# First half of an output projection as seven half-size products, with weight sums added in DRAM

## The chip, the cores and the metric

One core of a Trainium2 chip runs the whole layer. The metric is the device time of one execution in microseconds (us). Names of engines: PE is the matmul engine (PEld its weight load), DVE the vector engine, ACT the scalar engine, POOL and SP the two engines that here mostly issue transfers.

## The reference

One layer of a decoder with three parallel branches (256 positions, width 2048). What matters here is the end: three gated branches are merged, multiplied by a 2048 x 2048 matrix, normalised and added to the input.

```python
def hybrid_layer(x, mem, ...):
    h = rms_norm(x, pre_g)
    proj = h @ w_in
    a_u, a_v, a_g, b_x, b_g, x_q, x_g, gate_logits = jnp.split(proj, splits, axis=-1)
    y_a = spatial_gating(a_u, a_v, ...) * jax.nn.silu(a_g)
    y_b = s5_branch(b_x, ...) * jax.nn.silu(b_g)
    y_x = memory_cross_attention(x_q, rms_norm(mem, mem_g), xa_wk, xa_wv) * jax.nn.silu(x_g)
    ys = jnp.stack([y_a, y_b, y_x], axis=2)
    branch = jnp.einsum('bsnc,ncd->bsnd', ys, w_branch)
    gates = jax.nn.sigmoid(gate_logits.reshape(bsz, seq, N_BRANCH, D_MODEL))
    merged = jnp.sum(gates * branch, axis=2)
    out = merged @ w_out
    return x + rms_norm(out, post_g)
```

`s5_branch` is a state-space layer: a projection of 64 small groups, a scan over the positions, a projection back.

## The kernel before

All matmuls take float32 values split in a high and a low part (type fp32r), and three matmuls (high x high, high x low, low x high) make one product. Activations are split once. Weights stream from DRAM: `load` issues a transfer of 128 x 2048 values (1 MB) on SP's queue into one of three `raw` buffers; `split` makes of each half of it a high part (a cast on ACT, L92) and a low part (a subtraction on DVE, L93), in one of four `hl` buffers; then PE uses them. `tm_quarter` (L215) takes one such 1 MB quarter, 512 rows of a weight by 512 columns, and runs 24 matmuls with 512 columns each: 4 blocks of 128 rows, two halves of the 256 tokens (`tb`), three part products.

PE's instructions stand in the order in which the code is written. On the other engines a scheduler orders the instructions of the whole program by priority and by the time at which its own model sees them ready; each engine then works strictly in that order, and an instruction that waits holds up those behind it.

The layer begins with the state-space input: eight pieces of `start` (x and the first weights) are loaded by SP, then `w_bx`, the query weights `w_xq`, and so on. The state-space work itself (`s5_main`) runs beside the large matmuls: PE's part of it, and the helpers, are issued by `pump` after each block of weights. Its operands come by POOL's queue: `s5_load` loads a block `sb` of 128 KB (L531), `s5_prep` scales it on ACT into `B` (L543), and from the third block on adds its upper half to `B` by an adding transfer (L548):

```python
        a.activation(out=B4, in_=rw, func=AF.Copy, scale=sgn)
        ...
            g.dma_start(out=B4[64:P].bitcast(F32), in_=rw[64:P], accum_op=ALU.add)
```

At the end, the last branch is merged over four column blocks c (`w_br`, 2 quarters each), and `merge_t(c)` transposes the merged rows (`mt`) and splits them into `mm`, 16 blocks of 128 rows by 256 tokens. Then the output projection: three column blocks of 512 (4 quarters each, into one `acc` tile for both token halves), 256 columns from `w_out3[0]` (the 96 narrow matmuls of L1041), and the last 256 columns, whose four half buffers are split while the narrow matmuls run (`wks`; its first quarter in two pairs `wh`, `wl` of 512 columns); they are used by 48 matmuls for token half 0, then 48 for token half 1. `evac_out` squares each result on ACT, for the norm (L1003), and multiplies it by `gpost` on DVE (L1006). After the last square sum, `finish` scales, adds x and sends.

Of the kernel before, what the change touches and what calls it, by code (L numbers as in the profile page):

```python
# [9 lines left out]
F32 = mybir.dt.float32  # L10
# [8 lines left out]
P = 128  # L19
# [24 lines left out]
def trunk(ctx: ExitStack, tc: tile.TileContext, I, out):  # L44
# [109 lines left out]
    class Plain:  # L154
# [5 lines left out]
        def stationary(self, h, tb):  # L160
            return self.t[:, h, tb::2] if self.turn else self.t[:, h, tb * P:(tb + 1) * P]

    def norm_split(src, gv, dst, k0):
        for k in range(len(dst)):
            kk = k0 + k
            r = src[:, k * T:(k + 1) * T].rearrange("p (c b) -> p c b", c=2)
            hi, lo = dst[k].half(0), dst[k].half(1)
            a.activation(out=hi, in_=r, func=AF.Copy, scale=gv[:, kk:kk + 1])
            v.scalar_tensor_tensor(out=lo, in0=r, scalar=gv[:, kk:kk + 1],  # L169
                                   in1=hi.bitcast(F32), op0=ALU.mult, op1=ALU.subtract)  # L170
# [20 lines left out]
        pe.matmul(ps, lhsT=hl.stationary(0, tb), rhs=two(wl), start=False, stop=False)  # L191
        pe.matmul(ps, lhsT=hl.stationary(1, tb), rhs=two(wh), start=False, stop=last)  # L192

    bg = [iter(()), 0.0, []]

    def pump(credit):
        with tc.high_priority(offset=-BEHIND):
# [1 line left out]

    def pump_(credit):  # L200
        bg[1] += credit
        for gen in list(bg[2]):
            while True:
                c = next(gen, "end")
                if c == "end":
                    bg[2].remove(gen)
# [45 lines left out]
    for _ in range(NWARM):  # L252
        pe.matmul(wps, lhsT=wz[:, 0:P], rhs=wz, start=True, stop=True)

    xhl = [Pairs(xp.tile([P, 2, 2, P], F32R, name=f"x{k}")) for k in range(16)]
    u = slot("U", [P, 8, T])
    acc0 = [acc_tile(), acc_tile()]
    for pc in range(8):
# [551 lines left out]
    def merge(n, yhl, sink):  # L810
        for c in range(4):
            rate["tm"] = RT[6] + (0.33, 0.13, 0.0, 0.0)[c] * (n == 2)
            G = acc_tile()
            for kq in range(4):
                tm_quarter([G[:, 0], G[:, 1]], load(I["w_gate"][n, c, kq]), xhl, kq, 16)
            assert not bg[2] or n == 2 and c == 0
            Bp = acc_tile()
            sg = wk.tile([P, 2, 512], F32, tag="w0", name=nm("g"))
            for tb in range(2):
                a.activation(out=sg[:, tb], in_=G[:, tb], func=AF.Sigmoid, scale=rstd_x[:, tb:tb + 1])  # L820
            for kq in range(2):
                tm_quarter([Bp[:, 0], Bp[:, 1]], load(I["w_br"][n, c, kq]), Lane(yhl), kq, 8)
            sink(c, sg, Bp)
# [138 lines left out]
    def mm_tile(i):  # L962
        if i not in mm:
            mm[i] = slot(("H0", "H3", "U", "X0")[i], [P, 4, 2, T], F32R)
        return mm[i]

    def merge_t(c):
        yield None
        yield None
        for hf in range(2):  # L970
            tp = miscp.tile([P, 2, T], F32, tag="misc", name=nm("mt"))
# [6 lines left out]
            split_to(d[:, :, 0], d[:, :, 1], tp)  # L978
            if hf == 0:
                yield None  # L980

    for c in range(4):
        Bp = acc_tile()
        for kq in range(2):
            tm_quarter([Bp[:, 0], Bp[:, 1]], load(I["w_br"][1, c, kq]), yBs, kq, 8)
        for tb in range(2):
            d = sgB[tb][:, csl(c)]
            v.tensor_tensor(out=d, in0=Bp[:, tb], in1=d, op=ALU.mult)
            v.tensor_tensor(out=mg[tb][:, csl(c)], in0=mg[tb][:, csl(c)], in1=d, op=ALU.add)
# [11 lines left out]
    def sq_out(tb, ps, n, cs):  # L1001
        t = wk.tile([P, cs.stop - cs.start], F32, tag="w1", name=nm("sq"), padded_shape=[P, 512])
        a.activation(out=t, in_=ps, func=AF.Square, scale=D ** -0.5, accum_out=ssq[:, tb, n:n + 1])  # L1003

    def gated(dst, ps, lo_, hi_):
        v.tensor_tensor(out=dst, in0=ps, in1=gpost[:, 0, lo_:hi_], op=ALU.mult)  # L1006

    def evac_out(tb, ps, n, cs):
        sq_out(tb, ps, n, cs)
        if tb == 0 or n == 0:  # L1010
            gated(og[tb][:, cs], ps, cs.start, cs.stop)
        elif n == 1:
            gated(held[0], ps, 512, 1024)
        else:
            gated(ps, ps, cs.start, cs.stop)
            held.append(ps)

    held = [yp.tile([P, 512], F32, tag="y", name="held")]
    for n in range(3):
        acc = acc_tile()  # L1020
        for kq in range(4):
            tm_quarter([acc[:, 0], acc[:, 1]], load(I["w_out"][n, kq]), mhl2, kq, 16)
            if (n * 4 + kq) in (1, 4, 7):
                dst, src = late.pop(0)
                nc.sync.dma_start(out=dst, in_=src)
        for tb in range(2):
            evac_out(tb, acc[:, tb], n, csl(n))

    def tm_k(ps, wh, wl, k, tb):
        tm_mm(ps, wh, wl, mhl2[k], tb, k == 0, k == 15)  # L1030

    acc = acc_tile()
    for kh in range(2):
        raw = load(I["w_out3"][0, kh])
        for hf in range(2):
            wh, wl = split(raw[:, hf * 1024:(hf + 1) * 1024])
            for k in range(4):
                kk, ks = kh * 8 + hf * 4 + k, slice(k * T, (k + 1) * T)
                for i, (h, w) in enumerate(((0, wh), (0, wl), (1, wh))):
                    for tb in range(2):  # L1040
                        pe.matmul(acc[:, tb, 0:T], lhsT=mhl2[kk].stationary(h, tb), rhs=two(w[:, ks]),  # L1041
                                  start=kk == 0 and i == 0, stop=kk == 15 and i == 2)
    for tb in range(2):
        evac_out(tb, acc[:, tb, 0:T], 3, slice(1536, 1792))
    v.tensor_reduce(out=ss, in_=ssq[:, :, 0:4], axis=AX.X, op=ALU.add)
    v.tensor_scalar(out=ss, in0=ss, scalar1=EPS, scalar2=None, op0=ALU.add)
    a.activation(out=warm, in_=ss[:, 0:1], func=AF.Sqrt)
# [4 lines left out]
    for kh in range(2):  # L1052
        raw = load(I["w_out3"][1, kh])
        for hf in range(2):
# [147 lines left out]
```

## Time and profile before

| | |
|---|---|
| median of 3 runs | 907.83 us (907.59 to 908.53) |
| profiled execution | 908.71 us, its span 907.0 us |
| mean granted PE clock | 0.997 |
| PE busy | 896.6 us, 4896 matmuls |
| DVE, ACT busy | 760.7 us, 573.0 us |
| loaded and stored | 195.30 MB, mean 215 GB/s |

The span is from the first to the last instruction of the profiled execution. A busy share is an average over stages with different limits. In rows of the trace the first column is the start (or the stretch) in us from the start of the span, then comes the duration, the engine and line, the operation, and what it writes and reads; in brackets is how long the engine was idle before it and whose end it waited for. Rows of PE overlap, since matmuls are pipelined: their pitch is the distance of their starts.

### The profile page before, as it was taken

What the parts mean: (1) busy time and instruction counts of PE and PEld (TensorE: products, weight loads), DVE (VectorE), ACT (ScalarE), POOL (GpSimd) and SP (SyncE); (2) the same over time, 40 slices, a digit from 0 to 9 for tenths busy, and PEclk for the clock granted to TensorE, in tenths of its full rate; (3) what the DMA queues carried; (4) which work ended last, traced back from release to release, by engine and by line L of the source; (5) the groups of instructions that cost most, each with busy time, mean ns of one, the idle gap of its engine ahead of it and who ended that gap; (6) DMA issues with size and microseconds to landing.
All of it is one profiled execution on the core that took longest, in us unless ns stands there. A gap on an engine that the chain in (4) does not pass through costs nothing.

```text
span 907.0 us, 13070 instructions
## 1 busy us (share of the span) xinstructions
PE 896.6 (99%) x4896; PEld 797.2 (88%) x4896; DVE 760.7 (84%) x1188; ACT 573.0 (63%) x980; POOL 50.8 (6%) x80
## 2 busy tenths in 40 slices
PE   8999999999999999999999999999999999999996
PEld 7999898899888888889999888888988889998896
DVE  6899877977887999999797799999997967875554
ACT  7586655876667677685545667777666556544452
POOL 1000000100000111110000001110000000000000
PEclk9999999999999999999999999999999999999998
DMA  9877665653565666765655565566566566557542
GB/s 340 327 280 277 257 240 195 203 185 141 186 201 196 204 225 228 287 203 195 223 195 186 195 203 203 197 205 245 195 216 213 189 236 213 201 186 279 197 175 93
DMA packets 32864, 195.30 MB, mean 215 GB/s; under 512 B 4257, under 2 KB 6817, under 8 KB 11041
## 3 DMA queue, kind: packets, MB, share of 16 engines
q1 hardware_dynamic: 28000, 185.81, 57.4%
q0 software_dynamic: 3936, 6.16, 3.2%
q10 hardware_dynamic: 864, 2.49, 0.7%
q8 instruction: 38, 0.62, 0.3%
q14 instruction: 26, 0.21, 0.1%
HBM read 190.39 MB, written 2.10 MB: 212 GB/s over the span
## 4 chain that ended last, share of the span: by engine, by line
PE 89%; DVE 6%; DMA 2%; issue 1%; ACT 1%; SPq 0%; DVEq 0%; ACTq 0%
PE acc L190 19%; PE acc L192 19%; PE acc L191 19%; PE acc L174 17%; PE acc L179 9%; DVE hl L93 2%; DMA M<-mem 2%; PE acc L1041 1%; PE y L639 1%; PE bu L577 1%; DMA st<-start 1%; DVE H L169 1%; ACT hl L92 1%; PE po L758 1%; PE sc L724 1%
## 5 line engine op out<-in xcount | busy, mean ns | idle before, releaser
L93 DVE TENSOR_TENSOR hl<-raw,hl 128x1024 fp32r<-128x1024 f32 x319 | 388.1, 1220 | 108.7 <-ACT hl L92 107.0
L92 ACT CAST hl<-raw 128x1024 fp32r<-128x1024 f32 x319 | 331.4, 1045 | 210.8 <-PE acc L192 131.0
L174 PE MATMUL acc<-x,hl 128*128 128x512 f32 x736 | 218.7, 383 | 1.0 <-DVE x L169 1.0
L190 PE MATMUL acc<-hl,x 128*128 128x512 f32 x448 | 170.7, 381 | 0.0
L191 PE MATMUL acc<-hl,x 128*128 128x512 f32 x448 | 169.8, 379 | 0.0
L192 PE MATMUL acc<-hl,x 128*128 128x512 f32 x448 | 169.8, 379 | 0.0
L179 PEld LDWEIGHTS acc<-x,hl 128*128 128x128 f32 x736 | 137.0, 190 | 18.9
L179 PE MATMUL acc<-x,hl 128*128 128x256 f32 x736 | 139.0, 274 | 0.0
L174 PEld LDWEIGHTS acc<-x,hl 128*128 128x128 f32 x736 | 113.5, 193 | 2.9 <-ACT hl L92 1.8
L190 PEld LDWEIGHTS acc<-hl,x 128*128 128x128 f32 x448 | 84.7, 189 | 13.6 <-issue 2.5
L192 PEld LDWEIGHTS acc<-hl,x 128*128 128x128 f32 x448 | 84.7, 189 | 12.0
L191 PEld LDWEIGHTS acc<-hl,x 128*128 128x128 f32 x448 | 84.8, 189 | 11.2
L190 PE MATMUL acc<-hl,H 128*128 128x512 f32 (+1 forms) x180 | 68.2, 379 | 0.0
L191 PE MATMUL acc<-hl,H 128*128 128x512 f32 (+1 forms) x180 | 67.8, 377 | 0.0
L192 PE MATMUL acc<-hl,H 128*128 128x512 f32 (+1 forms) x180 | 67.8, 377 | 0.0
L174 PE MATMUL acc<-H,hl 128*128 128x512 f32 x192 | 57.4, 381 | 0.0
L548 POOL DMA_DIRECT2D B<-sb x30 | 25.4, 847 | 452.0 <-ACT B L543 410.8
L383 DVE TENSOR_TENSOR p<-bu,E 128x512 f32<-128x512 f32 x64 | 41.8, 684 | 1.3 <-PE bu L577 1.0
L615 DVE TENSOR_TENSOR_SCAN p<-s5r,p 128x256 f32<-128x256 f32 x64 | 41.3, 681 | 0.6
L179 PEld LDWEIGHTS acc<-H,hl 128*128 128x128 f32 x192 | 36.1, 189 | 5.7 <-DVE hl L93 0.8
L190 PEld LDWEIGHTS acc<-hl,H 128*128 128x128 f32 x180 | 34.0, 189 | 4.9 <-issue 0.4
L192 PEld LDWEIGHTS acc<-hl,H 128*128 128x128 f32 x180 | 34.0, 189 | 4.7
(276 smaller groups left out, 1244.3 us busy)
## 6 DMA issues: line engine op xcount, KB each, us to landing
raw<-w_gate SPq DMA_DIRECT2D x48, 1024.0 KB, 4.8
raw<-w_br SPq DMA_DIRECT2D x24, 1024.0 KB, 4.8
raw<-w_out SPq DMA_DIRECT2D x16, 1024.0 KB, 4.8
raw<-w_xq SPq DMA_DIRECT2D x8, 1024.0 KB, 4.8
raw<-wk SPq DMA_DIRECT2D x8, 1024.0 KB, 4.8
raw<-wv SPq DMA_DIRECT2D x8, 1024.0 KB, 4.8
raw<-w_xg SPq DMA_DIRECT2D x8, 1024.0 KB, 4.9
raw<-w_av SPq DMA_DIRECT2D x8, 1024.0 KB, 5.3
```

What stands on the lines that cost most here:

```text
L92: a.copy(out=hi, in_=src)
L93: v.tensor_tensor(out=lo, in0=src, in1=hi.bitcast(F32), op=ALU.subtract)
L169: v.scalar_tensor_tensor(out=lo, in0=r, scalar=gv[:, kk:kk + 1], in1=hi.bitcast(F32), op0=ALU.mult, op1=ALU.subtract)
L174: pe.matmul(ps, lhsT=wh, rhs=hl.moving_both(), start=k == 0, stop=False)
L179: pe.matmul(h, lhsT=wl, rhs=hl.moving(0), start=False, stop=k == nk - 1)
L190: pe.matmul(ps, lhsT=hl.stationary(0, tb), rhs=two(wh), start=first, stop=False)
L191: pe.matmul(ps, lhsT=hl.stationary(0, tb), rhs=two(wl), start=False, stop=False)
L192: pe.matmul(ps, lhsT=hl.stationary(1, tb), rhs=two(wh), start=False, stop=last)
L383: v.tensor_tensor(out=o, in0=i0, in1=i1, op=op)
L548: g.dma_start(out=B4[64:P].bitcast(F32), in_=rw[64:P], accum_op=ALU.add)
L577: pe.matmul(bu[:, ri, :], lhsT=B4[:, ri, :], rhs=two(U4), start=True, stop=True)
L615: v.tensor_tensor_scan(out=p2[:, ri], data0=rb, data1=p1[:, ri], initial=0.0, op0=ALU.mult, op1=ALU.add)
```

## The change

The first 1024 of the 2048 output columns are computed in another way. Let A be the merged activations (256 tokens by 2048), cut into token halves and row halves of the weight, and B the weight's first 1024 columns, cut into four quarters of 1024 rows by 512 columns. Instead of eight products of quarters there are seven (Strassen's method), each with 128 tokens, 1024 rows and 512 columns: 24 matmuls of 512 columns (`product`). Four of the seven take sums of weight quarters (`wsum`), and four take sums of activation quarters (S1 to S4). The results are put together by additions.

The sums of weights are formed in DRAM by transfers that POOL issues: for each `wsum`, 2 MB, two copies of 1 MB and four adding transfers of 0.5 MB. In the code their generator `weight_sums` is stepped by `pump` from the first `merge` on, with six steps between two transfers. The other 512-column block (`normal`) and the narrow columns (`narrow`) stand between the products. Two products take weight quarters that are loaded early into tiles `xr`, which take the place of the activation tiles `x`; so do `gpost` and x.

```diff
+    dram = ctx.enter_context(tc.tile_pool(name="dram", bufs=1, space=bass.MemoryType.DRAM))
+    wsum = [[dram.tile([P, 2048], F32, name=f"wsum{i}{k}") for k in range(2)] for i in range(4)]
+
+    def weight_sums():
+        w = I["w_out"]
+        for i, (base_, add) in ((0, (w[0, 0:2], w[1, 0:2])), (2, (w[1, 0:2], w[1, 2:4])),
+                                (1, (wsum[2], w[0, 0:2])), (3, (wsum[1], w[0, 2:4]))):
+            for k in range(2):
+                yield from steps(6)
+                g.dma_start(out=wsum[i][k], in_=base_[k])
+            for k in range(2):
+                for c in range(2):
+                    yield from steps(6)
+                    sl = slice(c * 1024, (c + 1) * 1024)
+                    g.dma_start(out=wsum[i][k][:, sl], in_=add[k][:, sl], accum_op=ALU.add)
+
+    bg[3].append(weight_sums())
     merge(2, yX, sink_first)
...
 def merge_t(c):
...
             split_to(d[:, :, 0], d[:, :, 1], tp)
+            lo_, up = tp[:, :, 0:P], tp[:, :, P:T]
+            if c < 2:
+                a.copy(out=r21[:, k], in_=up)
+                v.tensor_tensor(out=r3[:, k], in0=lo_, in1=r21[:, k], op=ALU.subtract)
+                split_to(S3[:, k, 0], S3[:, k, 1], r3[:, k])
+            else:
...
+                tt(t[:, 0], r21[:, k], up, ALU.subtract)
+                stt(t[:, 1], r3[:, k], -1.0, up, ALU.mult, ALU.subtract)
+                tt(t[:, 2], lo_, t[:, 1], ALU.add)
+                split_to(S1[0][:, k, 0], S1[0][:, k, 1], t[:, 0])
...
+    def early(src, i0):
+        ts = [xp.tile([P, 512], F32, tag=f"x{i0 + k}", name=nm("xr")) for k in range(4)]
+        for k in range(4):
+            nc.sync.dma_start(out=ts[k], in_=src[:, k * 512:(k + 1) * 512])
+        return ts
...
     for c in range(4):
         Bp = acc_tile()
         for kq in range(2):
             tm_quarter([Bp[:, 0], Bp[:, 1]], load(I["w_br"][1, c, kq]), yBs, kq, 8)
+        first_raws.append(early(I["w_out"][0, c], 4 * c))
...
-    for n in range(3):
-        acc = acc_tile()
-        for kq in range(4):
-            tm_quarter([acc[:, 0], acc[:, 1]], load(I["w_out"][n, kq]), mhl2, kq, 16)
...
+    def product(ps, form, raws_):
+        for kq in range(2):
...
+                for k in range(2):
+                    kk, sl = kq * 4 + hf * 2 + k, slice(k * 512, (k + 1) * 512)
+                    f = form[kk]
+                    pe.matmul(ps, lhsT=f(0), rhs=two(wh[:, sl]), start=kk == 0, stop=False)
+                    pe.matmul(ps, lhsT=f(0), rhs=two(wl[:, sl]), start=False, stop=False)
+                    pe.matmul(ps, lhsT=f(1), rhs=two(wh[:, sl]), start=False, stop=kk == 7)
+            pump(0.0)
...
+    normal(0)
+    product(X, a11, first_raws[0:2])
+    normal(1)
+    spread("g", I["g_post"][0].broadcast_to([P, D]), 0)
+    normal(2)
...
+    product(Y, a12, first_raws[2:4])
...
+    normal(3)
...
+    product(X, forms(S2[0][:, k] for k in range(8)), wsum[1])
...
+    narrow(0)
...
+    product(Z, forms(S1[0][:, k] for k in range(8)), wsum[0])
...
+    narrow(1)
...
+    product(Y, forms(S3[:, k] for k in range(8)), wsum[2])
...
+    tt(s3, Y, s2, ALU.add)
+    tt(c22, s5, s3, ALU.subtract)
+    sq_out(1, c22, 1, csl(1))
+    gated(held[0], c22, 512, 1024)
+    product(Z, forms(S4[k // 2][:, k % 2] for k in range(8)), w_o[1, 2:4])
+    tt(s5, Z, s5, ALU.add)
+    tt(s5, s5, s2, ALU.subtract)
...
+    product(X, a22, wsum[3])
+    tt(s3, X, s3, ALU.add)
+    sq_out(1, s3, 0, csl(0))
+    gated(og[1][:, csl(0)], s3, 0, 512)
```

Where the scheduler puts these instructions is seen in each engine's order. On POOL, near the start of the program, the rows of before are these (`ones` is a small constant, `sb` the first blocks of the state-space layer, whose first COPY waits for a cast on ACT):

```order
L311 MEMSET ones_1104 128x128
L530 COPY sb_1575<-H_21_363 128x1
L530 COPY sb_1604<-H_21_363 128x1
L531 DMA sb_1575<-s5b 128x256
L531 DMA sb_1604<-s5b 128x256
L531 DMA sb_1648<-s5b 128x256
```

In the change the same MEMSET is followed at once by the transfers of `weight_sums`; 16x16384 is a copy of 1 MB, 128x1024 an adding transfer of 0.5 MB:

```order
L318 MEMSET ones_1104 128x128
L858 DMA wsum_2405<-w_out 16x16384
L858 DMA wsum_2406<-w_out 16x16384
L863 DMA wsum_2405<-w_out 128x1024 x2
L863 DMA wsum_2406<-w_out 128x1024 x2
L858 DMA wsum_2409<-w_out 16x16384
L858 DMA wsum_2410<-w_out 16x16384
```

Then come four more adds, and after them, still on POOL:

```order
L858 DMA wsum_2407<-wsum_2409 16x16384
L858 DMA wsum_2408<-wsum_2410 16x16384
L863 DMA wsum_2407<-w_out 128x1024 x2
L863 DMA wsum_2408<-w_out 128x1024
L537 COPY sb_1575<-H_21_363 128x1
L537 COPY sb_1604<-H_21_363 128x1
L863 DMA wsum_2408<-w_out 128x1024
L538 DMA sb_1575<-s5b 128x256
L538 DMA sb_1604<-s5b 128x256
```

So all 24 transfers moved to the program's start, and `sb` from behind the MEMSET to behind 18 of them. An add waits for the copy into its tile, the copy of a `wsum` tile for the adds to it, and the first two copies wait for nothing. The orders of PE, DVE, ACT and SP are the same as before up to the last stages.

At the end of the program DVE's order before has the splits of the last 256 columns (`wl` twice, then `hl_8306`, `hl_8311` and `hl_8314`) among those of the narrow columns (`hl_8231` and `hl_8258`):

```order
L93 TENSOR_TENSOR hl_8202<-raw_8173,hl_8202 128x1024
L93 TENSOR_TENSOR wl_8299<-raw_8296,wh_8298 128x512
L93 TENSOR_TENSOR wl_8303<-raw_8296,wh_8302 128x512
L93 TENSOR_TENSOR hl_8231<-raw_8229,hl_8231 128x1024
L93 TENSOR_TENSOR hl_8258<-raw_8229,hl_8258 128x1024
L1006 TENSOR_TENSOR M_1023_7738<-acc_8037,gpost 128x512
L93 TENSOR_TENSOR hl_8306<-raw_8296,hl_8306 128x1024
L1006 TENSOR_TENSOR acc_8037<-acc_8037,gpost 128x512
L93 TENSOR_TENSOR hl_8311<-raw_8309,hl_8311 128x1024
L93 TENSOR_TENSOR hl_8314<-raw_8309,hl_8314 128x1024
```

In the change most of them stand behind the addition that reads the last product (`sn_8389<-acc_7821`), and the second `wl` behind the sum of the squares (TENSOR_REDUCE):

```order
L93 TENSOR_TENSOR hl_8471<-raw_8460,hl_8471 128x1024
L390 TENSOR_TENSOR sn_8176<-sn_8176 128x512
L93 TENSOR_TENSOR hl_8499<-raw_8489,hl_8499 128x1024
L1062 TENSOR_TENSOR M_1037_7817<-sn_8176,xr_8001 128x512
L390 TENSOR_TENSOR sn_8389<-acc_7821,sn_8389 128x512
L93 TENSOR_TENSOR wl_8492<-raw_8489,wh_8491 128x512
L93 TENSOR_TENSOR hl_8504<-raw_8502,hl_8504 128x1024
L93 TENSOR_TENSOR hl_8507<-raw_8502,hl_8507 128x1024
L1062 TENSOR_TENSOR M_1038_7818<-sn_8389,xr_8000 128x512
L1171 TENSOR_REDUCE sm_7820<-sm_7819 128x2
L93 TENSOR_TENSOR wl_8496<-raw_8489,wh_8495 128x512
```

The first `wl` has moved behind the last product, the second one to the end of the list; PE needs the second after the first.

More of the change, by code (lines that the diff above doesn't have):

```diff
@@ L192, in tm_mm, with steps @@
         pe.matmul(ps, lhsT=hl.stationary(1, tb), rhs=two(wh), start=False, stop=last)
-    bg = [iter(()), 0.0, []]
+    bg = [iter(()), 0.0, [], []]
+    def steps(n):
+        for _ in range(n):
+            yield None
     def pump(credit):
@@ L201, in pump_ @@
         bg[1] += credit
-        for gen in list(bg[2]):
+        for gens, gen in [(z, gen) for z in bg[2:] for gen in z]:
             while True:
@@ L253, in trunk @@
         pe.matmul(wps, lhsT=wz[:, 0:P], rhs=wz, start=True, stop=True)
-    xhl = [Pairs(xp.tile([P, 2, 2, P], F32R, name=f"x{k}")) for k in range(16)]
+    xhl = [Pairs(xp.tile([P, 2, 2, P], F32R, tag=f"x{k}", name=f"x{k}")) for k in range(16)]
     u = slot("U", [P, 8, T])
@@ L1032, in trunk, with spread, part @@
-    acc = acc_tile()
-    for kh in range(2):
+    post = {}
+    def spread(key, src, i0):
+        post[key] = early(src, i0)
+    def part(key, lo_, hi_):
+        return post[key][lo_ // 512][:, lo_ % 512:(hi_ - 1) % 512 + 1]
+    def gated(dst, ps, lo_, hi_):
+        v.tensor_tensor(out=dst, in0=ps, in1=part("g", lo_, hi_), op=ALU.mult)
+    XY = acc_tile()
+    X, Y = XY[:, 0], XY[:, 1]
+    N = acc_tile()
+    a11 = [mhl2[k].half2(0) for k in range(8)]
+    a12 = [mhl2[k + 8].half2(0) for k in range(8)]
@@ L1034, in trunk, with forms, normal, narrow @@
+    def forms(tiles):
+        return [(lambda h, t=t: t[:, h]) for t in tiles]
+    def normal(kq):
+        tm_quarter([N[:, 0], N[:, 1]], load(I["w_out"][2, kq]), mhl2, kq, 16)
+    c3 = []
+    def narrow(kh):
+        if not c3:
+            c3.extend(bup.tile([P, 512], F32, tag="bu", name=nm("oacc")) for _ in range(2))
         raw = load(I["w_out3"][0, kh])
@@ L1040, in trunk, with snap_tile @@
                     for tb in range(2):
-                        pe.matmul(acc[:, tb, 0:T], lhsT=mhl2[kk].stationary(h, tb), rhs=two(w[:, ks]),
+                        pe.matmul(c3[tb][:, 0:T], lhsT=mhl2[kk].stationary(h, tb), rhs=two(w[:, ks]),
                                   start=kk == 0 and i == 0, stop=kk == 15 and i == 2)
-    for tb in range(2):
-        evac_out(tb, acc[:, tb, 0:T], 3, slice(1536, 1792))
+            pump(0.0)
+    def snap_tile():
+        return wk.tile([P, 2, 512], F32, tag="w0", name=nm("sn"))
@@ new lines, in trunk @@
+    w_o = I["w_out"]
+    normal(0)
[3 more added lines that the diff above has]
+    normal(2)
+    sn = snap_tile()
+    s1, c11 = sn[:, 0], sn[:, 1]
+    a.copy(out=s1, in_=X)
+    product(Y, a12, first_raws[2:4])
+    tt(c11, s1, Y, ALU.add)
+    sq_out(0, c11, 0, csl(0))
+    gated(og[0][:, csl(0)], c11, 0, 512)
+    normal(3)
+    spread(0, I["x"][0], 4)
+    sq_out(0, N[:, 0], 2, csl(2))
+    sq_out(1, N[:, 1], 2, csl(2))
+    gated(og[0][:, csl(2)], N[:, 0], 1024, 1536)
@@ L1064, in trunk @@
                 wks += [(wh[:, k * T:(k + 1) * T], wl[:, k * T:(k + 1) * T]) for k in range(4)]
-    at = [bup.tile([P, 512], F32, tag="bu", name=nm("oacc"))[:, 0:T], acc[:, 1, T:2 * T]]
+    at = [c3[tb][:, T:2 * T] for tb in range(2)]
     ro = small([P, 2])
@@ L1098, in trunk @@
             for hf in halves_:
-                g.tensor_tensor(out=og[1][:, hf], in0=og[1][:, hf], in1=xo[1][:, hf], op=ALU.add)
+                g.tensor_tensor(out=og[1][:, hf], in0=og[1][:, hf], in1=part(1, hf.start, hf.stop), op=ALU.add)
             for hf in halves_:
```

83 lines of the change are left out of this document (52 added, 31 removed).

## The prediction

> **What bounds the kernel now.** I read the page first: the span, who is busy, and by what the chain that ended last is made up.
>
> ```profile
> span 907.0 us, 13070 instructions
> PE 896.6 (99%) x4896; PEld 797.2 (88%) x4896; DVE 760.7 (84%) x1188; ACT 573.0 (63%) x980; POOL 50.8 (6%) x80
> PEclk9999999999999999999999999999999999999998
> PE 89%; DVE 6%; DMA 2%; issue 1%; ACT 1%; SPq 0%; DVEq 0%; ACTq 0%
> ```
>
> TensorE works from end to end at full clock, and the chain is 89% PE. So a matmul taken away is worth its whole pitch, and a pause of PE costs its whole length. The next view, stretches of 10 us, says where there is room for more transfers.
>
> ```profile
> core 0: us, PE busy (x) PEld busy (x) DVE busy (x) ACT busy (x) POOL busy (x), PEclk, DMA share, GB/s
> 0.00:10.00 10.00, 7.58 (x25) 4.63 (x26) 3.18 (x9) 5.17 (x13) 3.29 (x12) 1.00 0.78 246
> 10.00:20.00 10.00, 10.00 (x61) 9.14 (x61) 9.33 (x19) 9.00 (x20) 0.00 (x0) 1.00 1.03 411
> 20.00:30.00 10.00, 10.00 (x64) 9.20 (x63) 7.75 (x13) 7.04 (x12) 0.00 (x0) 1.00 0.99 392
> 30.00:40.00 10.00, 10.00 (x63) 9.21 (x62) 9.52 (x32) 5.58 (x8) 0.00 (x0) 1.00 0.75 273
> 40.00:50.00 10.00, 10.00 (x63) 9.21 (x62) 10.00 (x57) 6.36 (x11) 1.60 (x4) 1.00 0.77 274
> ```
>
> The columns before the last name the share of the 16 DMA engines. From 10 to 30 us they are full, 392 to 411 GB/s; until 50 us they moved 2.46 + 4.11 + 3.92 + 2.73 + 2.74 = 16 MB. This is the stretch into which the change puts its transfers, as the order of POOL shows: all 24 of them stand right behind the MEMSET of `ones`, the first two with nothing to wait for. POOL's rows and ACT's, in order of time:
>
> ```profile
> 3.83 0.21 POOL L311 MEMSET ones<- 128x128 f32 x1
> 45.66 0.30 POOL L530 COPY sb<-H 128x1 f32<-128x1 f32 x2 [41.62 <-ACT H L168]
> 46.16 1.30 POOL L531 DMA_DIRECT2D sb<-s5b  x2 [0.20 <-POOL sb L530]
> 151.91 0.88 POOL L548 DMA_DIRECT2D B<-sb  x1 [49.45 <-ACT B L543]
> ...
> 8.63 0.51 ACT L168 ACTIVATE x<-st,xv 128x256 fp32r<-128x256 f32 x1 [1.44 <-DMA st<-start]
> 13.47 0.51 ACT L168 ACTIVATE x<-H,xv 128x256 fp32r<-128x256 f32 x1 [0.95 <-DMA H<-start]
> 51.61 0.90 ACT L543 ACTIVATE B<-sb,sm 128x256 fp32r<-128x256 f32 x2
> 52.42 1.05 ACT L92 CAST hl<-raw 128x1024 fp32r<-128x1024 f32 x1
> 54.62 1.05 ACT L92 CAST hl<-raw 128x1024 fp32r<-128x1024 f32 x1 [1.15 <-PE acc L179]
> ```
>
> Two things are to be seen. At 8.63 and 13.47 us ACT waits for the start loads, so they have no lead. And at 51.61 us ACT needs `sb`, loaded by POOL at 46.16; behind it on ACT stand the casts without which PE has no weights. In the change ACT's order is the same up to the last stages, but POOL issues `sb` only behind 6 of the 8 copies and all 12 of the adds that belong to them.
>
> **The change part by part.** *Matmuls.* 8 quarters of 24 matmuls become 7 products of 24: 24 fewer. The pitch is that of rows 26 matmuls apart; the last pass has its own:
>
> ```profile
> 782.76 0.38 PE L190 MATMUL acc<-hl,yB 128*128 128x512 f32 x1
> 788.37 0.38 PE L192 MATMUL acc<-hl,yB 128*128 128x512 f32 x1
> ...
> 893.68 0.28 PE L190 MATMUL acc<-wh,H 128*128 128x256 f32 x1
> 898.92 0.28 PE L192 MATMUL acc<-hl,X 128*128 128x256 f32 x1
> ```
>
> (788.37 - 782.76) / 26 = 0.216 us; 24 of them are **-5.2 us**, all on the path. The last pass has 47 steps in 5.24 us, 0.11 each.
>
> *The tail on DVE.* The splits of the last 256 columns stood under the narrow matmuls; now they stand behind the last product. These are the durations:
>
> ```profile
> 782.22 1.22 DVE L93 TENSOR_TENSOR hl<-raw,hl 128x1024 fp32r<-128x1024 f32 x1
> 783.35 1.29 DVE L989 TENSOR_TENSOR M<-M,H 128x512 f32<-128x512 f32 x2
> 875.18 1.29 DVE L93 TENSOR_TENSOR wl<-raw,wh 128x512 fp32r<-128x512 f32 x2 [0.26 <-ACT wh L92]
> 890.39 0.15 DVE L1045 TENSOR_REDUCE sm<-sm 128x2 f32<-128x8 f32 x1
> ```
>
> A 1024 split blocks DVE 1.13 us (783.35 - 782.22), a 512 operation about 0.6. In the new order DVE waits at `sn<-acc` for the last product, then does that (0.6), the first `wl` (0.6), two `hl` (2.3), the gating (0.6), the reduce (0.15) and only then the second `wl` (0.65): 4.9 us. The pass of token half 0 needs the second `wl` after its first 6 matmuls, at about 1.3 + 0.7 = 2.0 us; it then waits to 4.9, and its other 42 matmuls end at 4.9 + 4.7 = 9.6 instead of 5.3. **+4.3 us**; the bounds are 0 (if the scheduled order hardly bites) and 6 (if the last `raw` is late too).
>
> *More splits and sums.* 7 products take 28 splits of 1024 where 16 stood: 12 × 1.13 = 13.6 us of DVE and 12 casts of about 1 us on ACT, and DVE gets some 35 operations of 256 and 512 elements for the factors and sums, about 15 us. In the last stage DVE had this room:
>
> ```profile
> 820.00:840.00 20.00, 20.00 (x98) 17.54 (x97) 10.38 (x10) 9.88 (x13) 0.00 (x0) 1.00 0.76 286
> 840.00:860.00 20.00, 20.00 (x94) 17.50 (x94) 11.00 (x10) 8.83 (x12) 0.00 (x0) 1.00 0.55 207
> 860.00:880.00 20.00, 20.00 (x105) 17.80 (x104) 11.61 (x11) 10.27 (x14) 0.00 (x0) 1.00 0.60 211
> ```
>
> It was busy 33 of 60 us, so 27 were free there, and a little more in the columns of `w_br` before. 29 us just go in; following the order row by row I find PE fed, since four `hl` buffers lie ahead: 0, bounds 0 and 4. If that cover goes, a product takes 4 × 1.13 + 3 × 0.6 = 6.3 us instead of 24 × 0.216 = 5.2.
>
> *Loads at the end.* First products take early tiles, loaded under `glu` and `w_br` by SP: 4 MB more over some 25 us. SP waits there for x tiles that the last gate has read; PE is past them by then. Cost 0, bounds 0 and 2. The later products need 1 MB per 2.6 us, and one such load lands in 4.8:
>
> ```profile
> raw<-w_out SPq DMA_DIRECT2D x16, 1024.0 KB, 4.8
> ```
>
> With three buffers that just holds; 0, bounds 0 and 3.
>
> *The sums in DRAM.* Nothing in before adds in DRAM. The nearest rows are POOL's own transfers, in two short windows (151.9 to 154.8, and 262 to 268 us): packets, MB, share of the 16 engines, then the landing times.
>
> ```profile
> q0 software_dynamic: 80, 0.07, 24.8%
> B<-sb POOLq DMA_DIRECT2D x1, 64.0 KB, 2.6
> ...
> q0 software_dynamic: 48, 0.13, 5.5%
> sb<-s5b POOLq DMA_DIRECT2D x1, 128.0 KB, 3.1
> ```
>
> A plain load of 128 KB occupies the engines 0.055 × 6 = 0.33 us, which is 2.6 us per MB. The adding transfer of 64 KB occupies them 0.248 × 2.9 = 0.72 us: 4 rows of 1 KB on each engine, 0.18 us a row, more than four times the 0.041 of a plain row. A new add has 8 rows of 4 KB per engine. Its lower end is a fixed price per row, 8 × 0.18 = 1.4 us; its upper end a price per byte, 8 × 0.72 = 5.8. I take half of each, 3.6 us, since nothing here separates them. Latency outside the transfer is about 2.6 - 0.7 = 1.9 us.
>
> Until `sb` lands: POOL free at 4.0; five latencies on the chain copy, add, copy, add, load (9.5) and some four issues (0.85 each, 3.4); 6 copies of 1 MB (15.7); 12 adds (43). That is 76 us with the engines to itself. SP's 16 MB take 41 us of the same engines; the chain's own pauses give room for some 17, so 24 more would make 100. Not all of that is needed before ACT's place, and an add that waits on memory may leave the engine to others, so I take **90**. ACT stands at 51.6 then, and PE has a lead: the cast at 54.62 waited for PE to free a buffer of four, so two more halves of 12 × 0.216 = 2.6 us lay between that moment and the use of what was cast at 52.42: it was needed at 59.8, took 2.2 for cast and split, and had 5.2 us to spare. The pause of PE is 90 - 51.6 - 5.2 = **+33 us**. Bounds: with adds at 1.4 us the chain ends between 50 and 74, and at 5.8 between 102 and 126: 0 to 17, and 45 to 69. The two copies and four adds left behind `sb` meet full `raw` buffers: **+2**, bounds 0 and 6.
>
> The Trainium skill, "DMA: Bandwidth & Descriptors", section "Anatomy of one DMA — SWDGE (gpsimd) path", fits such a transfer by 2.0 us plus its bytes at 436 GB/s, with no surcharge for adding. By it an add of 512 KB would be 3.2 us with its latency, and `sb` would land at an estimated 43 us, so ACT would not wait at all. This case's 64 KB add, 0.72 us on the engines where that rate gives 0.15, speaks against it.
>
> Sum against the profiled execution, 908.71 us (0.9 above the median of 907.83): 908.7 - 5.2 + 4.3 + 33 + 2 = 943, about **942** for a median.
>
> **The rivals.** *Starved start.* Adds are cheap (1.4 to 2.4 us) and `sb` lands at 60 to 75, but the start loads, without lead at 8 to 14 us, share full engines with the copies. 4 to 5 MB of POOL's transfers before 30 us, at 2.6 us each, delay PE by 10 to 13 us, and the `sb` wait adds little: 908.7 - 0.9 + 12 to 20, 920 to 928. For it: DMA share 1.03; against it: the dear row of 0.18 us.
>
> *Adds priced per byte.* `sb` lands at 110 to 126, PE pauses 53 to 69: 960 to 980. For it: the 1 KB row ran at only 91 GB/s over 16 engines; against it: part of that must be fixed.
>
> *Not slower.* The added rows run like plain rows and fit between SP's packets: chain 17 + 15.7 + 15.7 = 48 us, `sb` in time. It decides from landing below 57 us (51.6 + 5.2). Then the end stage alone counts: 908.7 - 0.9 = 907.8, or 903.5 if DVE's late `wl` costs nothing. Against it: 12 MB more beside 16 MB at 2.45 us per MB is 70 us by bytes alone.
>
> **How the numbers follow.** The main case (PE waits for ACT's `sb`, adds of 2.4 to 4.8 us, 928 to 960) has 0.50, around 942. The starved start has 0.22, the price per byte 0.23, and not slower 0.05, of which 0.03 faster. The range leaves out the fringe on both sides: 917 to 972. A difference under 0.2% (1.8 us) is about what these runs can't tell from none.
>
> **What would show it.** Right: POOL's adds fill 4 us to beyond 80; ACT waits tens of us on `sb` at its first `B`, with PE idle behind it and DMA share near 1 until then; PE idle about 3 us just after the last pass began; 24 fewer matmuls of 512. Wrong: `sb` lands before 57 us; or PE idle already at 8 to 35 us on `start` and little at `B`; or idle between products, where I put 0.

## The result and the profile after

The changed kernel takes 965.6 us (median of 4 runs, 963.9 to 967.2), beside 908.2 for the kernel before on the same chip (4 runs): a ratio of 1.063, 95% interval 1.061 to 1.066. It is slower, and by 23.6 us more than the 942 predicted. The profiled execution took 967.2 us. First the page's lines that answer to those of before: the span, the engines' busy time, the granted clock and the DMA share in 40 slices, POOL's DMA queue, and what the chain of waits is made of.

```profile
span 965.5 us, 13226 instructions
PE 913.4 (95%) x4872; PEld 806.3 (84%) x4872; DVE 789.5 (82%) x1248; ACT 591.9 (61%) x1022; POOL 68.0 (7%) x104
PEclk9799889999999999999999999999999999999997
DMA  9999986665544656585665565657566588556672
q0 software_dynamic: 6496, 22.94, 9.7%
PE 83%; DMA 11%; DVE 4%; issue 1%; ACT 1%; SPq 0%; POOL 0%; DVEq 0%; ACTq 0%
```

PE has 24 matmuls fewer and is yet busy 16.8 us longer; its granted clock is below 0.9 in slices 2, 5 and 6. DMA is now 11% of the chain, and the DMA row is full for five slices, to about 120 us. The stretches of 10 us from the start say the same in numbers:

```profile
0.00:10.00 10.00, 7.58 (x29) 4.70 (x30) 4.13 (x11) 5.72 (x13) 4.46 (x14) 1.00 0.92 321
10.00:20.00 10.00, 5.65 (x26) 4.91 (x25) 4.16 (x9) 3.87 (x8) 4.41 (x6) 0.83 0.91 302
20.00:30.00 10.00, 5.99 (x30) 5.24 (x29) 2.69 (x5) 1.93 (x4) 0.00 (x0) 0.80 1.03 238
30.00:40.00 10.00, 5.49 (x25) 4.43 (x23) 2.17 (x4) 1.94 (x4) 1.71 (x2) 0.84 1.02 361
40.00:50.00 10.00, 7.25 (x32) 6.34 (x32) 4.34 (x8) 3.87 (x8) 1.65 (x2) 0.67 1.03 284
```

PE was full from 10 us on in before; here it issues 25 to 32 matmuls in 10 us instead of 61 to 64, long before the first `sb` is wanted. Who keeps it waiting is seen in ACT's rows (start, duration, what it waited for), and what POOL does meanwhile in POOL's. A third fence has `memT`'s row in the kernel before, and the time from issue to landing of `w_bx`, before and after:

```profile
15.07 0.51 ACT L171 ACTIVATE x<-st,xv 128x256 fp32r<-128x256 f32 x1 [5.49 <-DMA st<-start]
...
26.00 0.51 ACT L171 ACTIVATE x<-H,xv 128x256 fp32r<-128x256 f32 x1 [6.28 <-DMA H<-start]
...
41.58 0.51 ACT L171 ACTIVATE x<-H,xv 128x256 fp32r<-128x256 f32 x1 [6.95 <-DMA H<-start]
...
72.06 1.99 ACT L92 CAST hl<-raw 128x1024 fp32r<-128x1024 f32 x2 [8.30 <-DMA raw<-w_bx]
...
88.57 0.91 ACT L171 ACTIVATE H<-M,xv 128x256 fp32r<-128x256 f32 x2 [7.09 <-DMA M<-memT]
...
100.11 0.51 ACT L550 ACTIVATE B<-sb,sm 128x256 fp32r<-128x256 f32 x1 [5.88 <-DMA sb<-s5b]
```

```profile
3.97 1.24 POOL L858 DMA_DIRECT2D wsum<-w_out  x2
...
89.14 0.51 POOL L537 COPY sb<-H 128x1 f32<-128x1 f32 x2 [17.28 <-ACT H L171]
...
90.11 1.45 POOL L538 DMA_DIRECT2D sb<-s5b  x2
```

```profile
45.09 0.90 ACT L168 ACTIVATE H<-M,xv 128x256 fp32r<-128x256 f32 x2
...
raw<-w_bx SPq DMA_DIRECT2D x4, 1024.0 KB, 14.5
...
raw<-w_bx SPq DMA_DIRECT2D x4, 1024.0 KB, 40.0
```

ACT waits for `start`, `w_bx` and `memT`, piece after piece, and only at the end 5.9 us for `sb`. The loads' queue tells how late they are: `raw<-w_bx` lands 40.0 us after its issue instead of 14.5, the four `H<-start` 24.0 instead of 10.9 (medians). POOL itself stands 17.3 us at the COPY ahead of `sb`, because ACT's `H` is late. So the wait for `sb` is the last link of a start that was late already.

One place serves as a ruler: POOL's second `ones`, which waits for a matmul (L321 before, L328 after), at 102.25 us before and 156.78 after. The two stretches up to it, of before and of after, hold the same 590 matmuls:

```profile
0.00:102.25 102.25, 99.83 (x590) 89.42 (x591) 90.61 (x265) 68.61 (x117) 5.96 (x18) 1.00 0.82 307
```

```profile
0.00:156.78 156.78, 117.96 (x590) 99.78 (x591) 93.73 (x271) 68.54 (x119) 23.72 (x42) 0.88 0.96 309
```

54.5 us are lost here. PE is idle 38.8 us instead of 2.4 (+36.4), and its busy time for the same work is 18.1 us longer. The granted clock was 0.50 in seven stretches, 37.55 us in all, in which PE was busy 29.41 us: half of that, 14.7 us, is an estimate of what the slow clock cost. What makes up the other 3.4 us of busy time isn't shown. POOL's queue took these shares of the 16 DMA engines in the two stretches:

```profile
q0 software_dynamic: 192, 0.52, 1.6%
```

```profile
q0 software_dynamic: 2752, 17.30, 42.8%
```

The balance of the engines closes: 0.428 x 156.78 = 67.1 us for POOL's queue, 65.5 more than before (0.016 x 102.25 = 1.6); their free time fell from 0.18 x 102.25 = 18.4 to 0.04 x 156.78 = 6.3 us, so 12.1 of it were used; 65.5 - 12.1 = 53.4 us, of 54.5. This is bookkeeping: it says that the other traffic cost nearly what it did before, and not yet why PE is late. The experiments below test that. Nor does a packet's time tell whether the engine itself or the memory behind it was slow.

After that the two programs run in step, 54 us apart, until the last branch; the end adds 4.0 (of 967.2 - 908.7 = 58.5, less 54.5).

The end, in PE's rows around the start of the last pass:

```profile
939.12 0.27 PE L193 MATMUL oacc<-wh,H 128*128 128x256 f32 x1
941.31 0.38 PE L194 MATMUL oacc<-wl,H 128*128 128x256 f32 x1 [1.92 <-DVE wl L93]
...
942.44 0.38 PE L193 MATMUL oacc<-wh,H 128*128 128x256 f32 x1 [0.30 <-ACT wh L92]
944.86 0.58 PE L194 MATMUL oacc<-wl,H 128*128 128x256 f32 x1 [2.04 <-DVE wl L93]
...
945.45 0.42 PE L193 MATMUL oacc<-wh,H 128*128 128x256 f32 x1
...
950.99 0.30 PE L195 MATMUL oacc<-hl,U 128*128 128x256 f32 x1
...
951.47 0.28 PE L193 MATMUL oacc<-hl,X 128*128 128x256 f32 x1
...
951.91 0.28 PE L194 MATMUL oacc<-hl,X 128*128 128x256 f32 x1
```

PE waits 1.92 + 0.30 + 2.04 = 4.3 us, just what was predicted. But from 945.45 to 950.99 the pitch is 0.213 (26 steps in 5.54) instead of the 0.11 of the last four (951.47 to 951.91): from 944.86 on 28 steps took 6.13 us where 3.1 would do, 3.0 us more.

### The profile page after: what moved, and what is told of

Same layout as the page of the kernel before. It is cut to its first block, busy times and chain, and to the rows that moved or that the text cites. A ratio compares the mean times of both kernels' runs of the same rounds, so it can differ in the third digit from the quotient of the medians.

```text
span 965.5 us, 13226 instructions
## 1 busy us (share of the span) xinstructions
PE 913.4 (95%) x4872; PEld 806.3 (84%) x4872; DVE 789.5 (82%) x1248; ACT 591.9 (61%) x1022; POOL 68.0 (7%) x104
## 4 chain that ended last, share of the span: by engine, by line
PE 83%; DMA 11%; DVE 4%; issue 1%; ACT 1%; SPq 0%; POOL 0%; DVEq 0%; ACTq 0%
PE acc L177 17%; PE acc L193 17%; PE acc L194 16%; PE acc L195 16%; PE acc L182 9%; DMA sp<-s5p 4%; DVE hl L93 2%; DMA M<-memT 2%; DMA M<-x 2%; DMA H<-start 1%; PE oacc L1110 1%; DMA sb<-s5b 1%; PE y L646 1%; PE bu L584 1%; PE po L761 1%
## 5 line engine op out<-in xcount | busy, mean ns | idle before, releaser
L177 PE MATMUL acc<-x,hl 128*128 128x512 f32 x736 | 228.2, 397 | 31.4 <-ACT hl L92 15.8
L182 PEld LDWEIGHTS acc<-x,hl 128*128 128x128 f32 x736 | 140.9, 196 | 26.5 <-DVE hl L93 6.6
L177 PEld LDWEIGHTS acc<-x,hl 128*128 128x128 f32 x736 | 118.8, 200 | 35.6 <-ACT hl L92 33.9
L182 PE MATMUL acc<-x,hl 128*128 128x256 f32 x736 | 144.1, 282 | 3.1 <-DVE hl L93 3.1
L177 PE MATMUL acc<-H,hl 128*128 128x512 f32 x192 | 57.4, 381 | 0.0
L193 PE MATMUL acc<-hl,H 128*128 128x512 f32 x144 | 54.9, 382 | 0.0
L194 PE MATMUL acc<-hl,H 128*128 128x512 f32 x144 | 54.6, 379 | 0.0
L195 PE MATMUL acc<-hl,H 128*128 128x512 f32 x144 | 54.6, 379 | 0.0
L182 PE MATMUL acc<-H,hl 128*128 128x256 f32 x192 | 36.9, 274 | 0.0
L193 PEld LDWEIGHTS acc<-hl,H 128*128 128x128 f32 x144 | 27.2, 189 | 4.0 <-issue 0.4
```

Source lines behind the costliest of these rows:

```text
L177: pe.matmul(ps, lhsT=wh, rhs=hl.moving_both(), start=k == 0, stop=False)
L182: pe.matmul(h, lhsT=wl, rhs=hl.moving(0), start=False, stop=k == nk - 1)
L193: pe.matmul(ps, lhsT=hl.stationary(0, tb), rhs=two(wh), start=first, stop=False)
```

## The experiments

Two theories stood at first. *Starved start*: the 24 transfers fill the 16 DMA engines, SP's first loads land late, and PE idles and runs at a low clock. *The wait for sb*, the prediction's own term: ACT's place is fixed, and what is lost is the time until `sb` gets through POOL's queue.

**The sums alone.** `weight_sums` was put into the kernel before, nothing else:

```diff
     mg = Lazy()
...
+    def weight_sums():
...
+    bg[3].append(weight_sums())
```

> The kernel before with the 24 transfers of weight_sums alone; their results are used by nothing, the output projection stays at eight quarters. The transfers stand on POOL where they stand in the change: right behind ones, with sb behind 18 of them. Both theories (starved start loads, or ACT's wait for sb) put the loss of 54 us into the start and so expect 908 + 54 = 962 us, with the start as in the change: ACT at its first B at 100 us, POOL's ones on DVE's side and the later stages shifted by 54 us. If the change's 58 us need the new end stage (rival: the loss is additive only by chance, or the new buffers cause it), the time is well under 950.

Measured: 962.25 us (962.0 to 962.5), ratio 1.060 (1.058 to 1.062). POOL's second `ones` is at 156.02. So 54.4 us are the transfers' price, with the old end stage and old buffers.

**The change without the sums.**

```diff
-    bg[3].append(weight_sums())
...
-    product(X, forms(S2[0][:, k] for k in range(8)), wsum[1])
+    product(X, forms(S2[0][:, k] for k in range(8)), w_o[0, 2:4])
...
```

> The change without weight_sums: the four products that take sums of weight quarters load plain quarters of w_out instead, so their values are not the reference's, while every load, split, matmul and addition of the last stage stays. Theory: the end stage costs +4.2 us (24 matmuls fewer give 5.2, the late second wl with its waits and the cold matmuls behind it take 7 to 8, small waits between products 1 to 2), so 912 us. The prediction's own sum for this part was 908.7 - 5.2 + 4.3 = 907.8. Rival: the end is slow only because the shifted program meets something else; then 903 to 908.

Measured: 911.9 us (911.1 to 912.2), ratio 1.0044 (1.0028 to 1.0061). The two parts add up: 54.4 + 4.0 = 58.4, of 57.4 measured in the change.

**`sb` out of the queue.**

```diff
         if q < 2:
-            g.tensor_copy(out=rw[:, 0, 0:1], in_=mhl[0].half(0)[:, 0, 0:1].bitcast(F32))
-        g.dma_start(out=rw, in_=I["s5b"][q])
+            nc.sync.dma_start(out=rw, in_=I["s5b"][q])
+        else:
+            g.dma_start(out=rw, in_=I["s5b"][q])
```

> The change with the first two sb loads on SP's queue, just ahead of the first wk load, so that no sb stands behind the sums; POOL issues all 24 transfers in a row. Theory of the starved start: the wait for sb was only 6 us at the end of a start that was already 43 us late, so 958 to 966 us, and memT's ACT work still comes near 88 us instead of 45. Rival, the term on record (+33 us of PE pause for sb): 925 to 935 us, with memT's work near 50 to 55 us.

Measured: 967.9 us (two runs), ratio 1.066 (1.064 to 1.068). Not even the 6 us came back. ACT's rows of this run:

```profile
89.05 0.91 ACT L171 ACTIVATE H<-M,xv 128x256 fp32r<-128x256 f32 x2 [7.94 <-DMA M<-memT]
...
107.37 2.10 ACT L171 ACTIVATE H<-M,xv 128x256 fp32r<-128x256 f32 x5 [9.27 <-DMA M<-memT]
...
130.96 0.90 ACT L551 ACTIVATE B<-sb,sm 128x256 fp32r<-128x256 f32 x2
```

`B` no longer waits for anything, and `memT` comes as late as in the change (88.57); its second part is waited for instead. The edit did more than move a load: SP issued the two `sb` only at 124.0 us, and ACT's order has `B` behind more casts. But nothing waits for `sb` any more and the time stays, so the wait for `sb` as the cause of the 33 us has fallen.

**Plain writes in place of adds, and copies alone.**

```diff
-                    g.dma_start(out=wsum[i][k][:, sl], in_=add[k][:, sl], accum_op=ALU.add)
+                    g.dma_start(out=wsum[i][k][:, sl], in_=add[k][:, sl])
```

This is the first of the two; the second leaves the 16 adds out.

> The change with the 16 adding transfers turned into plain ones of the same size and place (accum_op taken away), so the sums of weights are not formed. 0 to 157 us of the changed kernel held 65 us of engine time of POOL's new transfers; at the 2.6 us per MB of a plain load the 16 MB would be 42 us, of which 21 are the adds'. If an add costs more than a plain write, as the prediction had it (3.6 us instead of 1.3 per 0.5 MB), the gain is 16 x (2.8 - 1.3) = 24 us of the 54: about 942 us. If the bytes alone decide (rival), nothing changes: 965 us.

> The change with the 8 copies of 1 MB alone, the 16 adds left out (so the products take plain quarters). By engine time: 8 x 2.6 = 21 us less the 12 us that the start had free, 9 us of loss, and the end's +4: 921 us. If the lead of the first loads is what counts and not the sum of engine time (rival: any transfer ahead of the start loads costs its time, nothing is given back), 908 + 21 + 4 = 933 us. If sb behind the chain is what counts, it lands in time here: 912.

Measured: 944.9 us (943.3 to 946.4) and 935.5 us (934.8 to 936.3), ratios 1.040 (1.038 to 1.042) and 1.030 (1.028 to 1.032). The first came near what was expected (942), the second near what its rival had (933). POOL's queue in the first 150 us of the two kernels, and in the first 160 us of the change (packets, MB, share of 16 engines):

```profile
q0 software_dynamic: 2752, 17.30, 29.3%
```

```profile
q0 software_dynamic: 448, 8.91, 15.5%
```

```profile
q0 software_dynamic: 2752, 17.30, 41.9%
```

That is 44.0, 23.3 and 67.0 us of all 16 engines. A plain write of 0.5 MB is (44.0 - 23.3) / 16 = 1.3 us, an adding one (67.0 - 23.3) / 16 = 2.7. Adding doubles the price in engine time; neither the fixed price per row (1.4) nor the price per byte (5.8) of the small adds held, and the middle taken, 3.6, was too high.

In time, against the change without sums: copies +23.6, plain writes +9.3, adding +20.8. The copies cost all of their 21.7 us of engines (23.3 less the 1.6 of before's own transfers), and nothing is given back. The writes behind them cost less than their engine time: the plain ones 9.3 of 20.7 us (44.0 - 23.3), while making them adding ones costs 20.8 for 23.0 more (67.0 - 44.0). With the copies alone ACT doesn't wait for `sb` at all (`B` at 73.17 follows the row ahead of it), and yet the 23.6 us are lost. These are the stretches of the copies alone:

```profile
10.00:20.00 10.00, 3.52 (x18) 2.81 (x16) 1.25 (x3) 1.02 (x2) 0.49 (x1) 0.84 0.95 342
20.00:30.00 10.00, 2.90 (x8) 2.27 (x8) 1.18 (x2) 1.02 (x2) 0.98 (x2) 0.50 0.92 350
...
50.00:60.00 10.00, 9.89 (x60) 9.12 (x61) 9.77 (x28) 6.02 (x8) 0.00 (x0) 1.00 0.81 273
...
80.00:90.00 10.00, 10.00 (x63) 9.18 (x62) 9.96 (x19) 7.71 (x13) 0.00 (x0) 1.00 0.69 256
```

PE starves most from 10 to 30 us, and from 50 us on it works at its full pace with engines to spare (0.81, 0.69). It can't catch up, since it is the bound there. So free engine time behind the start gives back nothing that is lost; it only takes in transfers that come that late.

**POOL in the order of the code.** The scheduler had put all 24 transfers at POOL's head, though the code steps them between the blocks of the state-space part. Holding POOL to the code's order makes the interleaving real (transfers from 160 to 611 us):

```diff
-    ctx.enter_context(tc.manual_schedule(engines={mybir.EngineType.PE}))
+    ctx.enter_context(tc.manual_schedule(engines={mybir.EngineType.PE, mybir.EngineType.Pool}))
```

> The change with POOL also in the order in which the code is written: the 24 transfers then stand among the adding B transfers and the sb loads of the state-space part, from the third adding B on, not behind ones. Theory of the starved start: the start is that of before, and the transfers find 16 engines that are busy 0.5 to 0.6 of the time, so nothing is lost there; the end stage's +4 us is left: 912 us. Rival: an add holds the engines so long that B and sb come late in the middle, 24 delays of 1 to 2 us: 930 to 960 us. Under the prediction's own term for the wait (sb behind 18 transfers) it is also about 908 to 912.

Measured: 914.8 us (913.3 to 917.4), ratio 1.008 (1.006 to 1.010). Of the 54 us some 3 are left (914.8 - 911.9); the rest is hidden, with the same bytes and the same adds. The second `ones` is at 101.48 us (101.17 without sums). The prediction's own term would have given this too, so this run doesn't part the two theories; the copies alone do.

**The tail, in two ways.** Both keep POOL in order.

```diff
-                    split_to(wh, wl, src[:, i * 512:(i + 1) * 512])
+                    with tc.high_priority(offset=AHEAD):
+                        split_to(wh, wl, src[:, i * 512:(i + 1) * 512])
```

> The change with POOL in the order of the code, and with the split of the first half of the last quarter (the two wh, wl pairs) at high priority, so that both wl stand on DVE ahead of the last product's sn addition. The same transfers and sums as in the change. Theory: PE's two waits of 2 us on wl and the cold matmuls behind them (28 x 0.10 us) go: 914.8 - 4 - 3 = 908 us, as before. Rival: the clock's loss was not due to the pause, or the last product's own additions now come late and the end waits for them: only 2 to 4 us go, 911 to 913.

```diff
     product(Z, forms(S1[0][:, k] for k in range(8)), wsum[0])
...
-    narrow(1)
...
     product(X, a22, wsum[3])
...
+    narrow(1)
...
```

> The change with POOL in the order of the code, and with the second half of the narrow columns (48 matmuls, 5.2 us) moved from behind the fourth product to behind the last one, where before had it: the splits of the last 256 columns and the last product's additions then stand under it. Same computation. Theory: both waits on wl and the cold stretch go as with the high priority, 908 us or a little less; rival: the narrow columns' squares and gating now come late on ACT and DVE and delay finish as much: 911 to 914.

Measured: 909.5 us (907.8 to 910.6), ratio 1.001 (1.000 to 1.002), for the early `wl`; 914.7 us (910.9 to 915.4), ratio 1.007 (1.006 to 1.008), for the narrow columns last. The row of PE's longest wait in the last pass of the first; the 10 us of that pass in it, and in the changed kernel; then the row of PE's longest wait in the second:

```profile
890.83 0.38 PE L194 MATMUL oacc<-wl,H 128*128 128x256 f32 x1 [0.65 <-DVE wl L93]
```

```profile
890.00:900.00 10.00, 9.29 (x81) 8.92 (x80) 8.55 (x19) 4.66 (x9) 0.00 (x0) 1.00 0.08 30
```

```profile
940.00:950.00 10.00, 6.34 (x30) 5.97 (x31) 5.05 (x10) 3.87 (x7) 0.00 (x0) 0.71 0.01 2
```

```profile
890.71 0.38 PE L193 MATMUL oacc<-wh,H 128*128 128x256 f32 x1 [2.48 <-DVE M L1062]
```

With the early `wl` the pause shrinks from 4.3 to 0.65 us and the clock stays at 1.00 where it was 0.71. 5.3 of the 7 us came back. With the narrow columns last there is a new wait: the last pass writes the same `oacc` that DVE must first read for the gating (L1062), and that stands behind the splits. The rival's time, 911 to 914 us, is nearly met and the late gating is its reason, but what waits in this trace is PE, not `finish`. The trace is of an execution of 910.9 us; the four others took 913.3 to 915.4 us, at a mean granted clock of 0.995 instead of 0.998, and no trace shows where.

**Spreading the transfers, and the last pauses.** In the kernel with the early `wl`, PE still paused in the middle. POOL's, ACT's and PE's rows there, and two stretches of 10 us:

```profile
361.93 1.36 POOL L873 TENSOR_SCALAR_AFFINE_SELECT H<-H 128x1024 f32<-128x1024 f32 x1 [12.37 <-DMA H<-sg_wT]
...
363.75 0.92 POOL L555 DMA_DIRECT2D B<-sb  x1
364.33 0.94 POOL L538 DMA_DIRECT2D sb<-s5b  x1
```

```profile
374.46 0.51 ACT L550 ACTIVATE B<-sb,sm 128x256 fp32r<-128x256 f32 x1 [6.94 <-issue]
```

```profile
376.94 0.48 PE L193 MATMUL acc<-hl,x 128*128 128x512 f32 x1 [1.02 <-ACT hl L92]
...
378.21 0.48 PE L194 MATMUL acc<-hl,x 128*128 128x512 f32 x1 [0.78 <-DVE hl L93]
...
370.00:380.00 10.00, 8.20 (x35) 6.57 (x34) 5.27 (x9) 5.41 (x10) 2.32 (x3) 0.95 1.06 322
380.00:390.00 10.00, 10.00 (x53) 7.66 (x53) 8.96 (x13) 6.11 (x12) 0.00 (x0) 0.88 0.91 260
```

POOL, in order, waits 12.4 us for `sg_wT` with `B` and `sb` behind it; ACT then waits 6.9 us at the next `B`. The profile names no releaser for that wait ("issue"), but the `sb` that POOL issued at 364.33 took 10.1 us to land, beside a copy and an add of the sums and at a DMA share of 0.99 to 1.06. Here, in small, is the wait that the prediction had placed at the start.

```diff
-    g.affine_select(out=sg_wT, in_=sg_wT, pattern=[[0, 8], [1, P]], compare_op=ALU.is_ge, fill=0.0, base=0,
-                    channel_multiplier=-1)
...
     tm_rows(I["w_av"], xhl, vt, "x")
+    g.affine_select(out=sg_wT, in_=sg_wT, pattern=[[0, 8], [1, P]], compare_op=ALU.is_ge, fill=0.0, base=0,
+                    channel_multiplier=-1)
...
-  yield from steps(6)
+  yield from steps(7)
```

> The kernel with POOL in code order and the early wl splits, with two edits more: POOL's affine_select, which there waits 12.4 us for sg_wT with B and sb queued behind it, stands behind the w_av block, and the 24 transfers are 7 steps apart instead of 6. Same computation. PE paused 1.8 us at 377 us, when ACT waited 6.9 us for sb; if POOL's queue is the cause that goes: 909.5 - 1.8 = 907.7 us. If the engine time of the transfers is the cause (rival), the pause stays or moves: 909 to 910.

```diff
+                with tc.high_priority(offset=AHEAD):
-                tt(t[:, 0], r21[:, k], up, ALU.subtract)
+                    tt(t[:, 0], r21[:, k], up, ALU.subtract)
...
```

> The same, and the three subtractions and additions of merge_t for S1, S2 and S4 at high priority, so that the psum tile mt is free earlier. PE paused 1.3 us there (mt waits for sa). Expected: 907.7 - 1.3 = 906.4 us, a little under before. Rival: the splits that these operations pass come late instead and PE pauses at hl: 907 to 908.

> The end stage alone, at its best here: without the sums (four products take plain quarters of w_out, so the values are not the reference's), POOL ordered by the scheduler as in the change, with the early wl splits and the early sa operations. Ceiling of what seven products can bring: 911.9 without sums, less 3.5 of pause and 2.9 of cold matmuls, less 1.3 at mt: 904.2 us; from the other side 907.9 - 5.2 (24 matmuls) + 1.5 for pauses left over = 904.2. Rival: the gain is eaten elsewhere in the last stage, 906 to 908.

Measured: 905.9 us (905.7 to 906.3), ratio 0.9976 (0.9967 to 0.9986); with the early `sa` 905.55 us (904.6 to 905.9), ratio 0.9968 (0.9956 to 0.9980); without the sums 904.8 us (904.2 to 906.6), ratio 0.9964 (0.9954 to 0.9975). Spread, PE doesn't pause at all from 100 to 800 us, and 3.6 us came back, twice the pause that was seen (1.8). An estimate for the rest is the clock behind the pause, 0.95 and 0.88 in two stretches of 10 us: 0.5 + 1.2 = 1.7 us. How much is the moved select and how much the seventh step isn't told apart. The early `sa` took PE's pause of 1.33 at `mt` away but lengthened one at `hl` from 0.16 to 0.61; the two intervals overlap, so its own gain isn't established. In the kernel with the early `sa` the last pass waits for this:

```profile
885.17 0.38 PE L194 MATMUL oacc<-wl,H 128*128 128x256 f32 x1 [0.66 <-DVE wl L93]
```

This kernel, with all sums formed, beats the one before by 2.4 us (0.2 to 0.4%). It lies 0.8 us above the one without sums, whose end stage is the same but whose POOL is ordered by the scheduler; the two intervals overlap, so no price of the transfers is left that these runs could show.

## Why the prediction was right and wrong

The measured time lies in the range on record, 917 to 972 us, but not by the mechanism on record. The main case had PE wait for `sb`, at 928 to 960 us; 965.6 lies outside these bounds though the add's price, 2.7 us, lies inside the main case's. That the range holds is luck: it was drawn to take in most of the rivals as well. The sign that the prediction named for being wrong, PE idle already at 8 to 35 us on `start` and little at `B`, is what the trace shows. Term by term:

- *Matmuls, -5.2.* Right in number: 4872 instead of 4896. Their price wasn't measured by itself.
- *Tail on DVE, +4.3.* Right in its mechanism and as a pause (4.3). What was not in it is the clock afterwards, 3.0 us.
- *Splits and sums, 0.* Nearly: PE paused 1.3 us for `sa` and 0.2 for an `hl`, 1.5 within the bounds of 0 and 4.
- *Loads at the end, 0.* Right: `raw` lands in 4.8 us, and PE waits for none.
- *Price of an add, 3.6 us.* Measured 2.7, inside the bounds of 1.4 and 5.8. With it the prediction's own sum gives 12 x 0.9 = 11 us less, 931, further from what was measured.
- *PE pause for `sb`, +33.* This step failed. Its sum let SP's 16 MB delay POOL's chain by 24 us, but the chain delay SP's loads by nothing: "ACT stands at 51.6 then". The same transfers that delayed `sb` delayed everything that ACT does ahead of `sb`, by 43 us already at `memT` (88.57 against 45.09), and ACT waited only 5.9 us for `sb` itself. With `sb` taken out of the queue the time stayed. The landing, put at 90, was about 100 (`B` at 100.11), and even that is no sign of a right chain: POOL was ready for `sb`'s COPY at about 72 us and then stood 17.3 us for ACT.
- *Copies and adds behind `sb`, +2.* Too small: from 104 us to the ruler at 156.78 PE was idle 4.9 us (inside the bounds of 0 to 6, if all of it is theirs), at a mean granted clock of 0.90.
- *Starved start, the rival at 920 to 928.* Its mechanism was the true one. Its size was too small: it counted the 4 to 5 MB before 30 us alone and tied itself to cheap adds. In fact all of POOL's transfers compete until about 120 us, and the loss is their engine time less the 12 us that were taken from free time.
- *Price per byte, the rival at 960 to 980.* It holds the measured time, but by another way: the adds were cheaper than it says.

The parts, against the profiled before: 908.7 + 36.4 (idle at the start) + 18.1 (longer busy there, 14.7 of it by the clock) - 5.2 (as predicted) + 4.3 + 3.0 + 1.5 = 966.8, of 967.2.

## What to carry to other kernels

Transfers for later use, put where the engines are full and the first loads have no lead, can cost PE their whole engine time (here 23.6 us for the 21.7 of the copies), and spare time later doesn't pay it back; those that come after may cost less (9.3 us for 20.7 of plain writes). Count the engine time of all of them and what they delay, not only the wait for the item queued behind. Look at the order that a scheduler really gives a DMA-issuing engine: the code interleaved these transfers, the program did not, and restoring it was worth 51 us. A pause of the matmul engine can have a second price, the slow matmuls behind it.

## What was not expected of the hardware

After some pauses of a few microseconds the matmuls run at half pace. At the start, in the changed kernel, a group of four 512-column matmuls took 2.04 us right behind a pause of 4.35 us and 1.03 us a little later:

```profile
16.24 2.04 PE L177 MATMUL acc<-x,hl 128*128 128x512 f32 x4 [4.35 <-DVE x L172]
...
20.38 1.03 PE L177 MATMUL acc<-x,hl 128*128 128x512 f32 x4
```

It made an estimated 14.7 of the 54.5 us lost at the start and 3.0 of 7.3 us in the tail. Not every pause does it: in the tail the matmuls right behind the first wait, of 1.92 us, ran at their full pace, and so did those behind the wait of 2.48 us in the run with the narrow columns last. The Trainium skill, "TensorE: Matmul & The Clock Gate", "Part 1: The HAM clock gate (the "warmup" mystery)", says that an idle array falls back to half its clock and needs about 3.4 us of sustained work, in a window that runs freely, to come back. The halving agrees with the trace (0.213 against 0.11 us); the stretches at a granted clock of 0.50 were 3.4 us long or twice that in the changed kernel, and the tail's matmuls were slow for 6.1 us (944.86 to 950.99).

An adding transfer of 0.5 MB within DRAM took 2.7 us of the 16 engines, a plain one 1.3. A 64 KB add into the core's own memory had taken 0.72, so per byte the large one cost about half (5.4 against 11.5 us per MB).
